# Second-layer modulation on VectorE: closing operations one to a place, the gates turned by PE and stored as rows, the first loads one chunk earlier in the program

## Chip, core and metric

One core of one Trainium2 chip runs the whole program. The metric is the device time of one execution in microseconds; the time before is the median of three runs. PE is the matrix engine, DVE is VectorE, ACT is ScalarE, POOL is GpSimd, SP is SyncE, whose queue issues nearly all DMAs here.

## The reference

A two-layer diffusion backbone: 1024 latent tokens and 256 context tokens of width 1024. Each layer is a mixer and a gated convolutional feed-forward network, each between norms whose shift, scale and gate come from a modulation vector:

```python
mod_lat = (jax.nn.silu(c) @ w_mod[l] + b_mod[l])[:, None, :]
mod_ctx = (jax.nn.silu(c_ctx) @ w_mod[l] + b_mod[l])[None, None, :]
sh1, sc1, g1, sh2, sc2, g2 = jnp.split(mod_lat, 6, axis=-1)
...
h_lat = rms_norm(x, norm_pre_ffn[l]) * (1.0 + sc2) + sh2
x = x + g2 * rms_norm(conv_ffn(h_lat, ...), norm_post_ffn[l])

def conv_ffn(h, w_up, conv_w, conv_b, w_down):
    u = depthwise_conv3(h @ w_up) + conv_b
    a, g = jnp.split(u, 2, axis=-1)
    return (jax.nn.silu(g) * a) @ w_down
```

The change is about the modulation of the second layer (l = 1): six vectors of 1024 for the latent tokens and the first two (shift and scale) for the context, 8192 dot products of length 1024.

## The kernel before

Matrix products are made in fp32 from split operands: each is a high and a low part in fp32r, and every product is three matmuls (high by high, low by high, high by low). The feed-forward network of the first layer (`ffn_up` with `ctx` true) runs over 22 chunks j = 0 to 21 of 128 hidden channels and their 128 gates. Its latent part is a 2x2 block product with 7 instead of 8 block products (S1 to S4 and T1 to T4 are sums of weight and token blocks), the context tokens are multiplied plainly (`u_pc`). In a chunk PE runs, in this order: the context product with A11 and A12; A12 (on B21); S2 (into `u_v`); the context product with A21 and A22; S1; S3; A22; A11 of the next chunk; and S4, which closes the chunk's `u_g`. VectorE adds the pieces up (`f_u`, then `u_v<-u_g`, which the S4 product waits for, then the second `u_v`), and makes the outer taps of the convolution; ScalarE makes the middle tap (`f_t`), the high parts of the weights and the silu; POOL makes the weight sums (`w_s`) and the low parts. Each finished chunk, `f_t` of 640 KB, is stored to DRAM (`actd`); there is one buffer per `f_t`, so that ScalarE's first middle tap of the context in the next chunk waits for that store.

Beside this, a generator, `mod_second`, makes the modulation of the second layer on VectorE. The context manager `in_order` holds the compute engines (PE, ACT, DVE, POOL) to the order in which the code is written; SP's DMAs are put in order by the framework's scheduler, up to chunk 21. `modulation(n)` takes n steps of the generator, and is called at fixed **places** of a chunk, seven in each of the chunks 1 to 21: one in `gate_end`, three after the sum `f_u`, one after each of the two context convolutions, one before the S4 product; and one more after the loop. In chunk 0 it takes none.

The generator's steps are: four loads of inputs (two rows `c_row`, the first two weight pieces `m_raw`) and three small tables; ScalarE's silu of the two rows; 128 jobs, each one product of a weight piece of 128x512 with the row, summed along it into one column of `m_acc` (the rows with L364), which also issues the load of the piece two jobs later into the buffer just read; then the sum of the two halves and the two bias sums in one step; and in the last step the copies and products that make the four tiles `mod_0`, `mod_1`, `mod_3`, `mod_4`, the gates `m_gate`, and two DMAs that write the gates, which lie across partitions, number by number to `gated` in DRAM. That is 132 steps, the last in chunk 19.

The next stage, `ffn_down`, multiplies by `w_down`; its first loads (`d_rawB`, `d_rawA`, `d_t`) are issued while the last chunks run. The second layer reads `mod` and `gated` much later.

Of the kernel before, what the change touches and what calls it, by code (L numbers as in the profile page):

```python
# [11 lines left out]
F32 = mybir.dt.float32  # L12
# [3 lines left out]
OP = mybir.AluOpType  # L16
# [4 lines left out]
P = 128  # L21
D = 1024
KT = D // P
# [26 lines left out]
def vap(t, off, dims):  # L50

    b = t[:]
    return bass.AP(tensor=b.tensor, offset=b.offset + off, ap=[list(b.ap[0])] + [list(d) for d in dims])
# [15 lines left out]
class Trunk:  # L69
# [255 lines left out]
                self.mod[l, kind] = m  # L325


    def mod_second(self, hp, sp):

        nc, a = self.nc, self.a  # L330
        raw, row = (hp.tile([P, 1024], F32, name=n, tag="n_t22", bufs=2) for n in ("m_raw", "c_row"))
# [40 lines left out]
            yield  # L372
        t = acc[:, 0]
        nc.vector.tensor_tensor(out=t, in0=t, in1=acc[:, 1], op=OP.add)
        nc.vector.tensor_tensor(out=t[:, :16], in0=t[:, :16], in1=bias[:, :16], op=OP.add)
        nc.vector.tensor_tensor(out=t[:, 16:], in0=t[:, 16:], in1=bias, op=OP.add)
        yield
        for kind in (0, 1, 3, 4):
            m = self.mod[1, kind] = self.cp.tile([P, KT, 2], F32, name=f"mod1_{kind}")
            for s in range(2 if kind < 2 else 1):  # L380
                src = t[:, (0 if s else 16) + KT * kind:][:, :KT]
                if kind in (1, 4):
                    w = pre[:, KT * (kind // 3):][:, :KT]
                    nc.vector.scalar_tensor_tensor(out=m[:, :, s], in0=src, scalar=1.0, in1=w, op0=OP.add, op1=OP.mult)
                else:
                    nc.vector.tensor_copy(m[:, :, s], src)
        nc.vector.tensor_tensor(out=gts, in0=vap(t, 16 + 2 * KT, ((3 * KT, 2), (1, KT))),
                                in1=post.rearrange("p (a b) -> p a b", a=2), op=OP.mult)
        for gi in range(2):
            nc.sync.dma_start(self.gated[1, gi, 0].rearrange("(k p) -> p k", p=P), gts[:, gi])  # L390


    def load_gates(self, l, gi, kinds, sp):
# [1186 lines left out]
    def ffn_up(self, l, src, ctx, x_src, x_dst, hp, pp, tp, es, ups, beside):  # L1580


        nc, a = self.nc, self.a
# [194 lines left out]
        with self.in_order(*self.compute, behind=l == 1), ExitStack() as loads:  # L1778
            sp, cw, sums = second_front() if l == 1 else up_front()

            down = iter(())
            mods = self.mod_second(hp, sp) if ctx else iter(())

            def modulation(n):
                for _ in range(n if j else 0):
                    next(mods, None)

            for j in range(FK):
# [79 lines left out]
                conv_start(t1[:, :SEQ], V, j + FK)  # L1868
                next(down, None)
                modulation(1)  # L1870
                product(Z, ("S4",), "B22", False, True)
                if "p1" in ahead:
                    st["p1"] = ahead.pop("p1")
# [1058 lines left out]
```

## Time and profile before

| what | value |
|---|---|
| median of three runs | 3279.52 us (3276.45 to 3287.17) |
| the profiled execution, whole | 3285.08 us |
| its span, first to last instruction | 3283.2 us |
| mean granted PE clock | 0.969 |
| first layer's up-projection, chunks 1 to 21 | about 1106 to 1635 us of the span |
| VectorE's 128 products for the modulation (L364) | 148.4 us busy, 1121.2 to 1568.6 us |
| packets under 512 B, whole execution | 26944 |

Times in rows of the profile are microseconds from the start of the span; a group's mean is in nanoseconds. In a row of the timeline the first number is the start, the second the duration; the brackets at its end hold how long the engine had been idle and what released it. "SPq" is a DMA issue of SP's queue, not the transfer. A row of the windows holds the stretch, its length, the busy time of PE, PE's weight load, DVE, ACT and POOL with the count of instructions, the granted clock, the DMA engines' mean busy share and GB/s.

### The profile page before, as it was taken

The numbers are of one execution on the slowest core, as the hardware profiler recorded it, in microseconds if no ns is written. First come the engines' busy times: TensorE is split into PE (matmuls) and PEld (weight loads), VectorE is DVE, ScalarE is ACT, GpSimd is POOL, SyncE is SP. The second block draws the span as 40 slices with busy tenths as digits, with TensorE's granted clock in tenths as the row PEclk, the third lists the DMA queues.
The fourth block names the chain that finished last, engine by engine and source line by source line (L and its number), as shares of the span: only waits on it lengthen the run. The fifth ranks groups of instructions, "written<-read, shape, count | busy, mean of one in ns | idle before, by whom it ended". The sixth has DMA issues, their size and how long they took to land.

```text
span 3283.2 us, 48708 instructions
## 1 busy us (share of the span) xinstructions
PE 3080.9 (94%) x18160; PEld 2551.2 (78%) x18160; DVE 2143.3 (65%) x3610; ACT 1506.6 (46%) x2693; POOL 1584.8 (48%) x1169
## 2 busy tenths in 40 slices
PE   7989999689998899999999989999998989999998
PEld 4867777478887688888788768889986768888787
DVE  4457666567775787878578652477775464555787
ACT  3323332366665444334344442566665543443443
POOL 1130111477773676776500111677775367777200
PEclk8999999699999899999999989999998989999999
DMA  7333112511114244444475672222224212222755
GB/s 251 110 101 119 41 37 64 180 30 63 58 55 155 87 146 156 141 140 149 124 250 200 224 226 108 70 64 63 61 72 163 91 64 84 78 89 84 252 195 180
DMA packets 212149, 396.13 MB, mean 121 GB/s; under 512 B 26944, under 2 KB 88896, under 8 KB 211912
## 3 DMA queue, kind: packets, MB, share of 16 engines
q1 hardware_dynamic: 202216, 359.46, 33.2%
q0 software_dynamic: 9696, 33.57, 2.6%
q8 instruction: 142, 2.33, 0.3%
q14 instruction: 95, 0.78, 0.1%
HBM read 314.28 MB, written 79.05 MB: 120 GB/s over the span
## 4 chain that ended last, share of the span: by engine, by line
PE 74%; DVE 11%; DMA 4%; ACT 4%; issue 4%; POOL 2%; SPq 0%; POOLq 0%; ACTq 0%; DVEq 0%
PE g_ps L139 20%; PE u_g L139 13%; PE d_ps L139 12%; PE u_v L139 10%; PE u_pc L139 3%; PE a_pv L139 2%; PE c_pv L139 2%; PE c_s L139 2%; PE c_pt L2560 2%; PE a_pt L1183 2%; DVE a_pl L1185 1%; PE o_ps L139 1%; PE a_s L139 1%; DMA d_rawB<-in_w_down 1%; DMA m_raw<-in_w_mod 1%
## 5 line engine op out<-in xcount | busy, mean ns | idle before, releaser
L147 POOL TENSOR_TENSOR rs_r<-rs_e,mhalf 128x1 f32<-128x1 f32 (+3 forms) x102 | 82.5, 810 | 839.3 <-DVE rs_e L146 422.6
L139 PE MATMUL d_ps<-d_Bl,d_Ah 128*128 128x512 f32 x704 | 276.7, 393 | 3.0 <-DVE d_Bl L1943 3.0
L139 PE MATMUL d_ps<-d_Bh,d_Ah 128*128 128x512 f32 x704 | 275.7, 392 | 2.9 <-ACT d_Bh L1942 1.5
L2543 POOL TENSOR_SCALAR c_p<-c_p,rl 128x640 f32<-128x640 f32 (+1 forms) x128 | 232.8, 1820 | 93.9 <-DVE rl L2542 62.4
L139 PE MATMUL d_ps<-d_Bh,d_Al 128*128 128x512 f32 x704 | 275.7, 392 | 1.5 <-DVE d_Al L1943 1.5
L1163 POOL TENSOR_SCALAR a_p<-a_p,rl 128x1280 f32<-128x1280 f32 (+1 forms) x80 | 242.2, 3030 | 62.6 <-DVE rl L1162 55.8
L139 PE MATMUL g_ps<-xh,w_hi 128*128 128x512 f32 (+1 forms) x640 | 257.0, 402 | 5.6 <-DVE hq L794 3.5
L139 PE MATMUL g_ps<-xh,w_lo 128*128 128x512 f32 (+1 forms) x640 | 238.0, 372 | 2.2 <-POOL w_lo L2443 2.2
L139 PE MATMUL g_ps<-xl,w_hi 128*128 128x512 f32 (+1 forms) x640 | 238.0, 372 | 0.0
L1185 DVE TENSOR_TENSOR a_pl<-a_pt,a_ph 128x512 fp32r<-128x512 f32 (+1 forms) x200 | 119.0, 602 | 88.1 <-ACT a_ph L1184 87.9
L364 DVE CUSTOM_DVE_ANT_0 m_raw<-m_raw,c_row 128x512 f32<-128x512 f32 x128 | 148.4, 1170 | 23.4 <-DMA m_raw<-in_w_mod 23.2
L1620 DVE TENSOR_TENSOR f_u<-u_v,f_p 128x512 f32<-128x512 f32 x88 | 60.4, 687 | 152.9 <-PE u_v L139 152.9
L139 PEld LDWEIGHTS d_ps<-d_Bl,d_Ah 128*128 128x128 f32 x704 | 132.8, 189 | 34.8 <-DVE d_Bl L1943 7.0
L139 PEld LDWEIGHTS d_ps<-d_Bh,d_Ah 128*128 128x128 f32 x704 | 132.8, 189 | 32.5 <-ACT d_Bh L1942 2.6
L1606 POOL TENSOR_TENSOR w_S4l<-w_s,w_S4h 128x512 fp32r<-128x512 f32 x44 | 57.2, 1301 | 207.5 <-ACT w_S4h L1605 207.5
L139 PEld LDWEIGHTS d_ps<-d_Bh,d_Al 128*128 128x128 f32 x704 | 132.9, 189 | 30.0 <-DVE d_Al L1943 2.9
L1184 ACT CAST a_ph<-a_pt 128x512 fp32r<-128x512 f32 (+1 forms) x200 | 102.0, 518 | 109.4 <-PE a_pt L1183 109.3
L2563 DVE TENSOR_TENSOR c_pl<-c_pt,c_ph 128x256 fp32r<-128x256 f32 (+1 forms) x256 | 113.0, 470 | 59.2 <-ACT c_ph L2562 58.0
L139 PE MATMUL g_ps<-w_hi,xh 128*128 128x512 f32 (+1 forms) x368 | 143.6, 390 | 5.5 <-DVE xh L2317 3.0
L139 PE MATMUL g_ps<-w_lo,xh 128*128 128x512 f32 (+1 forms) x368 | 138.2, 375 | 3.5 <-DVE w_lo L2304 2.4
L139 PEld LDWEIGHTS g_ps<-xh,w_lo 128*128 128x128 f32 x640 | 121.2, 189 | 25.2 <-POOL w_lo L2443 2.7
L139 PEld LDWEIGHTS g_ps<-xh,w_hi 128*128 128x128 f32 x640 | 121.6, 190 | 24.6 <-issue 7.6
(589 smaller groups left out, 10007.8 us busy)
## 6 DMA issues: line engine op xcount, KB each, us to landing
w_raw<-in_w_up SPq DMA_DIRECT2D x88, 512.0 KB
d_rawA<-actd SPq DMA_DIRECT2D x77, 512.0 KB
d_rawB<-in_w_down SPq DMA_DIRECT2D x74, 512.0 KB
m_raw<-in_w_mod SPq DMA_DIRECT2D x128, 256.0 KB
m_raw<-in_w_mod SPq DMA_DIRECT2D x48, 512.0 KB
actd<-f_t SPq DMA_DIRECT2D x22, 640.0 KB
actd<-f_t SPq DMA_DIRECT2D x22, 512.0 KB
vcd<-cv_st POOLq DMA_DIRECT2D x20, 512.0 KB, 2.9
```

The source lines that it names most:

```text
L139: return self.nc.tensor.matmul(out, lhsT, rhs, start=start, stop=stop, skip_group_check=True, **k)
L147: nc.gpsimd.tensor_tensor(out=r[:p, :n], in0=e[:p, :n], in1=self.mhalf[:p, :n], op=OP.pow)
L364: nc.vector.tensor_tensor_reduce(out=w, in0=w, in1=halves[1][n % 2], scale=1.0, scalar=0.0, op0=OP.mult, op1=OP.add, accum_out=acc[:, k, o ...
L1163: nc.gpsimd.tensor_scalar(Pt[:, :nk], Pt[:, :nk], rl, None, op0=OP.mult)
L1183: nc.tensor.transpose(pt[:, m, qt * P:(qt + 1) * P], Pt[:, kts[j + m] * P:(kts[j + m] + 1) * P], self.ident)
L1184: nc.scalar.copy(ph[:, j:j + n], pt[:, :n])
L1185: nc.vector.tensor_tensor(out=pl[:, j:j + n], in0=pt[:, :n], in1=ph[:, j:j + n].bitcast(F32), op=OP.subtract)
L1606: nc.gpsimd.tensor_tensor(out=lo, in0=part(j, name), in1=hi.bitcast(F32), op=OP.subtract)
L1620: nc.vector.tensor_tensor(out=out, in0=x, in1=y, op=OP.add)
L2543: nc.gpsimd.tensor_scalar(Pt[:, :n], Pt[:, :n], rl, None, op0=OP.mult)
L2560: nc.tensor.transpose(pt[:, j, :], Pt[:, (src + j) * P:(src + j + 1) * P], self.ident)
L2563: nc.vector.tensor_tensor(out=vap(pl, o, dims), in0=pt[:, :cnt], in1=vap(ph, o, dims).bitcast(F32), op=OP.subtract)
```

## The change

Four things. The two bias sums each get a step of their own, and so does each operation that makes the `mod` tiles; three of these tiles' copies go from VectorE to ScalarE. The gates are made first, turned by a PE transpose into a PSUM tile (`m_pt`), copied by ScalarE into a `c_row` buffer that is free by then, and stored as 16 rows of 128 numbers. And one step, the loads, is taken at the end of chunk 0. With it the generator has 141 steps after chunk 0, the last at the first place of chunk 21.

```diff
--- before.py
+++ after.py
@@ -325,7 +325,7 @@
                 self.mod[l, kind] = m
 
 
-    def mod_second(self, hp, sp):
+    def mod_second(self, hp, sp, tp):
 
         nc, a = self.nc, self.a
         raw, row = (hp.tile([P, 1024], F32, name=n, tag="n_t22", bufs=2) for n in ("m_raw", "c_row"))
@@ -372,22 +372,31 @@
             yield
         t = acc[:, 0]
         nc.vector.tensor_tensor(out=t, in0=t, in1=acc[:, 1], op=OP.add)
+        yield
         nc.vector.tensor_tensor(out=t[:, :16], in0=t[:, :16], in1=bias[:, :16], op=OP.add)
+        yield
         nc.vector.tensor_tensor(out=t[:, 16:], in0=t[:, 16:], in1=bias, op=OP.add)
         yield
+        nc.vector.tensor_tensor(out=gts, in0=vap(t, 16 + 2 * KT, ((3 * KT, 2), (1, KT))),
+                                in1=post.rearrange("p (a b) -> p a b", a=2), op=OP.mult)
+        yield
+        pt = tp.tile([P, 512], F32, name="m_pt", tag="n_pt", bufs=1)
+        nc.tensor.transpose(pt[:16, :P], gts.rearrange("p a b -> p (a b)"), self.ident)
+        yield
+        rows = halves[1][0][:16, :P]
+        nc.scalar.copy(rows, pt[:16, :P])
+        for gi in range(2):
+            nc.sync.dma_start(self.gated[1, gi, 0].rearrange("(k p) -> k p", p=P), rows[KT * gi:KT * gi + KT])
         for kind in (0, 1, 3, 4):
             m = self.mod[1, kind] = self.cp.tile([P, KT, 2], F32, name=f"mod1_{kind}")
             for s in range(2 if kind < 2 else 1):
                 src = t[:, (0 if s else 16) + KT * kind:][:, :KT]
+                yield
                 if kind in (1, 4):
                     w = pre[:, KT * (kind // 3):][:, :KT]
                     nc.vector.scalar_tensor_tensor(out=m[:, :, s], in0=src, scalar=1.0, in1=w, op0=OP.add, op1=OP.mult)
                 else:
-                    nc.vector.tensor_copy(m[:, :, s], src)
-        nc.vector.tensor_tensor(out=gts, in0=vap(t, 16 + 2 * KT, ((3 * KT, 2), (1, KT))),
-                                in1=post.rearrange("p (a b) -> p a b", a=2), op=OP.mult)
-        for gi in range(2):
-            nc.sync.dma_start(self.gated[1, gi, 0].rearrange("(k p) -> p k", p=P), gts[:, gi])
+                    nc.scalar.copy(m[:, :, s], src)
 
 
     def load_gates(self, l, gi, kinds, sp):
@@ -1779,7 +1788,7 @@
             sp, cw, sums = second_front() if l == 1 else up_front()
 
             down = iter(())
-            mods = self.mod_second(hp, sp) if ctx else iter(())
+            mods = self.mod_second(hp, sp, tp) if ctx else iter(())
 
             def modulation(n):
                 for _ in range(n if j else 0):
@@ -1868,6 +1877,8 @@
                 conv_start(t1[:, :SEQ], V, j + FK)
                 next(down, None)
                 modulation(1)
+                if j == 0:
+                    next(mods, None)
                 product(Z, ("S4",), "B22", False, True)
                 if "p1" in ahead:
                     st["p1"] = ahead.pop("p1")
```

What stands where after that. The first place is the start of chunk 1 on VectorE, from the product that closes chunk 0 (`f_t`, 128x1280); the rows L364 come in pairs, the product and the reading of its sum. Before:

```order
L1654 TENSOR_TENSOR f_t_11301<-f_t_11301,f_t_11300 128x1280
L1620 TENSOR_TENSOR f_u_11481<-u_v,f_p_11379 128x512
L364 ISA m_raw,m_acc<-m_raw,c_row 128x512
L364 ISA m_acc 128x1
L364 ISA m_raw,m_acc<-m_raw,c_row 128x512
L364 ISA m_acc 128x1
L1626 SCALAR_TENSOR_TENSOR f_t_11514<-u_pc,cw,f_t_11514 128x255
L1628 SCALAR_TENSOR_TENSOR f_t_11514<-u_pc,cw,f_t_11514 128x255
L364 ISA m_raw,m_acc<-m_raw,c_row 128x512
L364 ISA m_acc 128x1
L1626 SCALAR_TENSOR_TENSOR f_t_11513<-u_pc,cw,f_t_11513 128x255
L1628 SCALAR_TENSOR_TENSOR f_t_11513<-u_pc,cw,f_t_11513 128x255
```

and with the change:

```order
L1663 TENSOR_TENSOR f_t_11301<-f_t_11301,f_t_11300 128x1280
L1629 TENSOR_TENSOR f_u_11483<-u_v,f_p_11391 128x512
L364 ISA m_raw,m_acc<-m_raw,c_row 128x512
L364 ISA m_acc 128x1
L364 ISA m_raw,m_acc<-m_raw,c_row 128x512
L364 ISA m_acc 128x1
L364 ISA m_raw,m_acc<-m_raw,c_row 128x512
L364 ISA m_acc 128x1
L1635 SCALAR_TENSOR_TENSOR f_t_11516<-u_pc,cw,f_t_11516 128x255
L1637 SCALAR_TENSOR_TENSOR f_t_11516<-u_pc,cw,f_t_11516 128x255
L364 ISA m_raw,m_acc<-m_raw,c_row 128x512
L364 ISA m_acc 128x1
```

One product more stands ahead of the first context convolution (128x255), and all later ones have moved up by one place. SP's row for the loads of `c_row` and of the first two pieces is the same in both programs, behind the same four weight loads. On ScalarE the silu of the two rows stands ahead of the casts of w_A11h and w_A12h instead of behind them.

The second place is chunk 19 on VectorE, where the jobs end. Before, from the last product on:

```order
L364 ISA m_raw,m_acc<-m_raw,c_row 128x512
L364 ISA m_acc 128x1
L1626 SCALAR_TENSOR_TENSOR f_t_15458<-u_pc,cw,f_t_15458 128x255
L1628 SCALAR_TENSOR_TENSOR f_t_15458<-u_pc,cw,f_t_15458 128x255
L374 TENSOR_TENSOR m_acc<-m_acc 128x64
L375 TENSOR_TENSOR m_acc<-m_acc,m_tab 128x16
L376 TENSOR_TENSOR m_acc<-m_acc,m_tab 128x48
L1626 SCALAR_TENSOR_TENSOR f_t_15457<-u_pc,cw,f_t_15457 128x255
L1628 SCALAR_TENSOR_TENSOR f_t_15457<-u_pc,cw,f_t_15457 128x255
L386 COPY mod_0_15468<-m_acc 128x8 x2
L384 SCALAR_TENSOR_TENSOR mod_1_15471<-m_acc,m_tab 128x8 x2
L386 COPY mod_3_15474<-m_acc 128x8
```

then mod_4, m_gate and the three sums f_u, u_v, u_v. With the change:

```order
L374 TENSOR_TENSOR m_acc<-m_acc 128x64
L1635 SCALAR_TENSOR_TENSOR f_t_15459<-u_pc,cw,f_t_15459 128x255
L1637 SCALAR_TENSOR_TENSOR f_t_15459<-u_pc,cw,f_t_15459 128x255
L376 TENSOR_TENSOR m_acc<-m_acc,m_tab 128x16
L1635 SCALAR_TENSOR_TENSOR f_t_15458<-u_pc,cw,f_t_15458 128x255
L1637 SCALAR_TENSOR_TENSOR f_t_15458<-u_pc,cw,f_t_15458 128x255
L378 TENSOR_TENSOR m_acc<-m_acc,m_tab 128x48
L1629 TENSOR_TENSOR f_u_15488<-u_v,f_p_15312 128x512
L1629 TENSOR_TENSOR u_v<-u_g,f_u_15488 128x512
L1629 TENSOR_TENSOR u_v<-u_v,f_u_15488 128x512
L380 TENSOR_TENSOR m_gate<-m_acc,m_tab 128x16
```

The lump between the two convolutions and in front of f_u has become one small operation at each; the gates stand behind the sums that PE waits for. The rest on VectorE follows in chunk 20 (from its first context convolution; before, no row of the modulation was left there):

```order
L1635 SCALAR_TENSOR_TENSOR f_t_15674<-u_pc,cw,f_t_15674 128x255
L1637 SCALAR_TENSOR_TENSOR f_t_15674<-u_pc,cw,f_t_15674 128x255
L397 SCALAR_TENSOR_TENSOR mod_1_15648<-m_acc,m_tab 128x8
L1635 SCALAR_TENSOR_TENSOR f_t_15673<-u_pc,cw,f_t_15673 128x255
L1637 SCALAR_TENSOR_TENSOR f_t_15673<-u_pc,cw,f_t_15673 128x255
L397 SCALAR_TENSOR_TENSOR mod_1_15648<-m_acc,m_tab 128x8
L1629 TENSOR_TENSOR f_u_15704<-u_v,f_p_15525 128x512
```

and mod_4 in chunk 21, ahead of the convolution of `u_g`. On ScalarE the copies of `m_pt` and of mod_0 stand in chunk 20 between the casts of w_A12h and w_S2h, that of mod_3 ahead of the copy f_p. On PE the one new row, the transpose, stands in chunk 20 between the products A12 and S2. POOL's order is the same.

The third place is SP's queue around the gates' DMAs. Before:

```order
L349 DMA m_raw<-in_w_mod 128x512 x2
L1655 DMA actd<-f_t_15241 128x1280
L349 DMA m_raw<-in_w_mod 128x512
L1589 DMA w_raw<-in_w_up 128x1024
L390 DMA gated<-m_gate 128x8x1 x2
L1908 DMA d_rawB<-in_w_down 128x2x512
L1655 DMA actd<-f_t_15458 128x1280
L1908 DMA d_rawA<-actd 128x2x512
```

and with the change:

```order
L1598 DMA w_raw<-in_w_up 128x1024
L349 DMA m_raw<-in_w_mod 128x512 x2
L1664 DMA actd<-f_t_15243 128x1280
L1598 DMA w_raw<-in_w_up 128x1024
L1919 DMA d_rawB<-in_w_down 128x2x512
L389 DMA gated<-c_row 8x128 x2
L1664 DMA actd<-f_t_15459 128x1280
L1919 DMA d_rawA<-actd 128x2x512
```

The gates' two DMAs have gone from in front of the first load of `w_down` to behind it; they stay ahead of the store of chunk 19 (the first `actd` below them).

## The prediction

> **What bounds the kernel now.** I read the page first, for the engine that sets the end.
>
> ```profile
> PE 3080.9 (94%) x18160; PEld 2551.2 (78%) x18160; DVE 2143.3 (65%) x3610; ACT 1506.6 (46%) x2693; POOL 1584.8 (48%) x1169
> ```
>
> PE is busy 94% of the span, so an instruction of another engine costs time only where PE stands still for it. The change lies in the up-projection of the first layer. There I read the chain in order of time (start, length, what).
>
> ```profile
> 1159.06 2.87 PE u_pc L139 x24
> ...
> 1183.90 2.87 PE u_pc L139 x24
> ...
> 1592.13 11.29 DMA actd<-f_t
> ...
> 1611.16 2.87 PE u_pc L139 x24
> ...
> 1635.15 190.17 PE d_ps L139 x837
> ```
>
> The first row is the context product that opens chunk 3, the second that of chunk 4: a chunk is 24.84 us of PE. The third u_pc row opens chunk 21, 18 chunks after chunk 3. At 18 x 24.84 = 447.12 us it would stand at 1606.18; it stands at 1611.16. So **4.98 us are lost** between chunks 3 and 21, and the chain names a DMA of 11.29 us there. PE's timeline, taken in pieces from 1110 to 1615, shows where; the brackets hold PE's idle time and who ended it.
>
> ```profile
> 1130.12 0.50 PE L139 MATMUL u_g<-x_B220h,w_S4h 128*128 128x512 f32 x1 [0.26 <-DVE u_v L1620]
> 1156.04 0.50 PE L139 MATMUL u_g<-x_B220h,w_S4h 128*128 128x512 f32 x1 [0.79 <-DVE u_v L1620]
> 1580.57 0.50 PE L139 MATMUL u_g<-x_B220h,w_S4h 128*128 128x512 f32 x1 [1.95 <-DVE u_v L1620]
> 1608.14 0.50 PE L139 MATMUL u_g<-x_B220h,w_S4h 128*128 128x512 f32 x1 [2.39 <-DVE u_v L1620]
> ```
>
> These are the S4 products of chunks 1, 2, 19 and 20, each waiting for VectorE's sums. Chunks 3 to 18 show no idle at all. The last two, 4.34 us, are most of the 4.98; the rest is the restart after each. The places between are full, so the jobs themselves cost nothing today.
>
> **The closing lump, chunk 19.** VectorE's timeline there:
>
> ```profile
> 1572.31 0.99 DVE L374 TENSOR_TENSOR m_acc<-m_acc 128x64 f32<-128x64 f32 x1
> ...
> 1576.51 1.33 DVE L384 SCALAR_TENSOR_TENSOR mod<-m_acc,m_tab 128x8 f32<-128x8 f32 x2
> ...
> 1579.02 0.16 DVE L387 TENSOR_TENSOR m_gate<-m_acc,m_tab 128x16 f32<-128x16 f32 x1
> 1579.10 0.68 DVE L1620 TENSOR_TENSOR f_u<-u_v,f_p 128x512 f32<-128x512 f32 x1
> ```
>
> And the same stretch of the chunk before, where two products of the modulation stand in its place:
>
> ```profile
> 1547.46 1.22 DVE L364 CUSTOM_DVE_ANT_0 m_raw<-m_raw,c_row 128x512 f32<-128x512 f32 x1
> ...
> 1549.53 0.87 DVE L364 CUSTOM_DVE_ANT_0 m_raw<-m_raw,c_row 128x512 f32<-128x512 f32 x1
> ...
> 1551.09 0.69 DVE L1620 TENSOR_TENSOR f_u<-u_v,f_p 128x512 f32<-128x512 f32 x1 [0.69 <-PE u_v L139]
> ```
>
> In step with chunk 18 the sum f_u would start at 1551.09 + 24.84 = 1575.93; it starts at 1579.10, 3.17 us late, of which PE shows 1.95. Afterwards this chunk has one product less, the accumulator sum in that product's place, and one bias sum after each context convolution. A small operation took between 0.16 and about 1.3 us here, so I price each of the two at 1.3 us: from 1572.31, where the first pair of convolutions is done, plus 1.3, plus the second pair (0.48 each, as in the row at 1124.38 below), plus 1.3, gives f_u at 1575.87. That is in step, even at the dearest price. The 1.95 us go. The gate product stands behind the last sum PE waits for. In chunk 20 the two mod_1 operations take the same two places (2.6 us against 1.22 + 0.87 + 0.69 idle = 2.78): hidden. mod_4 stands in chunk 21 ahead of a convolution that waits for ScalarE anyway.
>
> **The gate's DMA, chunk 20.**
>
> ```profile
> 1579.20 1.00 SPq L390 DMA_DIRECT2D gated<-m_gate  x2
> DMA packets 2633, 1.70 MB, mean 68 GB/s; under 512 B 2128, under 2 KB 2128, under 8 KB 2632
> 1570.79 0.56 ACT L1623 ACTIVATE f_t<-u_pc,cw 128x256 f32<-128x256 f32 x1
> 1603.52 0.57 ACT L1623 ACTIVATE f_t<-u_pc,cw 128x256 f32<-128x256 f32 x1 [5.03 <-DMA actd<-f_t]
> ```
>
> Two issues of 4 KB write 2048 single numbers: in 1579 to 1604 the DMA view counts 2128 packets under 512 B. The 640 KB store of chunk 19 (on the chain at 1592.13) sits behind them for 11.29 us, ScalarE stands 5.03 us behind the store, and VectorE and PE behind ScalarE. A store without them:
>
> ```profile
> 1120.73 0.33 SPq L1655 DMA_DIRECT2D actd<-f_t  x1
> 1123.78 0.57 ACT L1623 ACTIVATE f_t<-u_pc,cw 128x256 f32<-128x256 f32 x1 [0.27 <-DMA actd<-f_t]
> ```
>
> It is down in 3.05 us. Afterwards the gates leave as 16 rows of 512 B, in SP's order behind a load of w_down and ahead of this store, ready some microseconds before it. The store, itself 1.95 us earlier, is issued at about 1590.2 and down at 1593.2; ScalarE needs it in step with its convolution of chunk 19 (1570.79 + 24.84) at 1595.6. The 2.39 us go too, with both restarts: **the term is -4.98 us**. The cover is 2.4 us wide; a landing time of 5.4 us would use it up, and every microsecond more would come back. Next late in chunk 20 is then nothing but PE. The row at 1635.15 says that what gained here is kept: 837 matmuls of the down-projection follow without a wait, and their loads are released by this stage's buffers.
>
> **What is added.**
>
> ```profile
> L296 PE MATMUL mod_pt<-ident,mod_rows 128*128 128x128 f32 x12 | 1.9, 282 | 0.7 <-ACT mod_rows L234 0.7
> 1565.57 0.62 ACT L1605 CAST w_S2h<-w_s 128x512 fp32r<-128x512 f32 x1 [3.02 <-POOL w_s L1599]
> ```
>
> One transpose on PE, in the full stretch of chunk 20: 0.16 us in a stream (1.9 / 12), 0.28 alone; I take **+0.28**. Its operand is a chunk's last fifth old by then, so it waits for nothing. The trace has no copy as small as ScalarE's four new ones; a 128x256 activation took 0.57 (row at 1603.52), so the copy out of PSUM and two of mod_0 are at most 1.7 us, and stand before w_S2h, where ScalarE idles 3.02: nothing. The fourth stands ahead of the copy f_p, behind which ScalarE waits for a convolution.
>
> **The loads a chunk sooner.** In SP's order the four loads keep their place, since the buffers that they fill are read until then; and
>
> ```profile
> 1115.00:1117.00 2.00, 2.00 (x15) 1.84 (x14) 0.80 (x1) 2.00 (x4) 0.25 (x1) 1.00 0.00 0
> 1117.61 1.15 ACT L344 ACTIVATE c_row<-c_row 128x512 f32<-128x512 f32 x2
> ```
>
> the DMA engines already stand empty before the first use. Worth nothing. What moves is each job, one place ahead: ScalarE's silu by two casts (the two products take 1.15 us, and POOL, which reads the casts next, has two sums to make first), and in chunk 1 a third product before the first context convolution.
>
> ```profile
> 1122.40 4.99 SPq L349 DMA_DIRECT2D m_raw<-in_w_mod  x3
> 1124.38 0.48 DVE L1626 SCALAR_TENSOR_TENSOR f_t<-u_pc,cw,f_t 128x255 f32<-128x255 f32 x1 [0.30 <-ACT f_t L1623]
> 1125.30 1.73 DVE L364 CUSTOM_DVE_ANT_0 m_raw<-m_raw,c_row 128x512 f32<-128x512 f32 x1
> 1139.35 1.58 DVE L364 CUSTOM_DVE_ANT_0 m_raw<-m_raw,c_row 128x512 f32<-128x512 f32 x1 [2.70 <-DMA m_raw<-in_w_mod]
> L364 DVE CUSTOM_DVE_ANT_0 m_raw<-m_raw,c_row x128: 680/1042/1807, 1121.2 to 1568.6; 128x512 f32<-128x512 f32 x128
> ```
>
> The last row has the product's shortest, median and longest time in ns. The third product's weights are issued at 1122.40. By the times of this stretch they are down some 2.3 us later, since VectorE took them at 1125.30 without a wait. It can start at about 1124.7 and ends near 1125.8, so the convolution comes 1.4 us later; a shorter wait in each later product gives part back, and I put chunk 1's S4 0.6 us later. Chunk 2's S4 is set by the wait at 1139.35, whose load stands behind a weight load on SP before and after, so it stays at 1156.04. PE has 0.79 us to spare there: 0.6 vanishes in it. From both sides: chunk 2's stall gone as well, -1.06 (its S4 comes 25.92 after that of chunk 1, against 24.84); or the last three products of chunk 1 at the longest, 1.81 us: 1124.7 + 3 x 1.81 + 4 x 0.48 + 2 sums of 0.7 = 1133.4, 3.3 later, of which chunk 2 has 0.79 and a restart of 0.3 to spare: +2.2. I take **+0.1**, near the rows of chunk 1 itself.
>
> The product took 0.87 us in chunk 18 and 1.73 in chunk 1. [...]
>
> **Sum.** -4.98 + 0.28 + 0.1 = -4.6 us. The profiled execution took 3285.08 us (span 3283.2 and 1.88 around it), so 3280.5; that execution was 5.56 above the median of the three runs, 3279.52, and against the median it is **3274.9**.
>
> **Rivals.**
> - *A wait takes the place of the DMA's* (0.12): the store still lands late in chunk 20, beside the first load of w_down, and only chunk 19's stall goes: -1.95, a restart of 0.32, + 0.28 + 0.1, about -1.9: 3277.6. For it: a load of 512 KB is issued ahead of the store. Against: it is the store's own 3.05 us that count by then, with 2.4 us of cover.
> - *Chunk 2 is relieved too* (0.12): the product in front of its convolution finds its weights earlier: -1.06 more, 3273.8. Against: SP's order there.
> - *Slower, the crowded second chunk* (0.05): the products stand one place closer to the start. If the six before chunk 2's S4 each wait for a POOL instruction and take 1.81 us instead of the median 1.04, its S4 comes 4.6 us later, and POOL, held by the last three of chunk 1 for as much (2.3 us), releases the weight load later that stands ahead of the wait at 1139.35: with PE's 0.79 spent, +6.1 in place of +0.1, net +1.4, 3280.9. It decides from a slip of 5.5 us in chunk 2. Against: chunks 3 to 18 run this very order without an idle PE.
> - *The change doesn't bring what it moves to PE's end* (0.05): the gain is waited for again at the end of the down-projection, where the chain is VectorE and DMA: 0, 3279.5. Against: those loads are released in order by what comes before.
>
> **How the numbers follow.** My forecast has 0.66. A measurement of this kernel can tell about 0.3%, 9.8 us, from no change, and every case is smaller. What falls outside comes from scatter: the three runs reach from 3.1 below to 7.7 above their median. From -4.6, another 5.2 us down makes it faster (0.08), 14 up slower (0.03); same 0.89. The range takes the rivals, 3273.8 to 3280.9, the dear end of chunk 1 (3277.0), and some 4 us of scatter around the middle of the cases: 3269 to 3283.
>
> **What would show it.** Right: no idle PE before the S4 products of chunks 19 and 20; u_pc rows 24.84 apart from chunk 3 to 20, and chunk 21's 25.1 after; some 2000 packets under 512 B fewer on the page; the store of chunk 19 down in 3 to 4 us; VectorE's small closing operations still up to 1.3 us each, but with f_u waiting for PE behind them. Wrong: idle PE over 1 us before S4 in chunk 1 or over 0.8 in chunk 2 beside full chunks 19 and 20 (the start gives it back); or ScalarE still waiting for actd in chunk 20.

## The result, and the profile after

| | before | this |
|---|---|---|
| median, 22 runs each | 3282.18 us (3274.78 to 3288.70) | 3276.26 us (3271.88 to 3283.20) |
| ratio | | 0.9985 (0.9979 to 0.9991) |
| profiled execution, whole / span | 3285.08 / 3283.2 us | 3275.59 / 3273.8 us |
| mean granted PE clock | 0.969 | 0.970 |

The ratio is -4.9 us (-3.0 to -6.9). The forecast was -4.6, and 3274.9 us against a median of 3279.52 in three runs. By the prediction's bound of 0.3% that is no change, though the interval leaves out zero. The spans differ by 9.4 us, but some 5 of these lie in front of chunk 0's S4 and behind the opening of chunk 21, where the two programs are nearly alike; I take them for scatter. So the comparison goes by stage.

The chain of waits of the changed kernel in order of time (start, length, what), in the stretch shown of before:

```profile
1156.58 2.87 PE u_pc L139 x24
...
1578.86 2.87 PE u_pc L139 x24
1581.73 2.75 PE u_g L139 x12
1584.48 0.11 PE m_pt L384
1584.59 2.77 PE u_v L139 x12
...
1603.85 2.87 PE u_pc L139 x24
...
1627.85 12.25 PE d_ps L139 x53
```

The first row opens chunk 3, the last u_pc row chunk 21: 447.27 us, where before took 452.10. The DMA of 11.29 us has left the chain, and so have all VectorE and ScalarE rows in front of 1603.85. The step from chunk 20 to 21, 1578.86 to 1603.85, is 24.99, with the transpose's 0.11 in it. The down-projection follows at 1627.85 without a wait.

PE's timeline, the S4 rows with an idle time in brackets, from chunk 0 on:

```profile
1102.53 0.47 PE L139 MATMUL u_g<-x_B220h,w_S4h 128*128 128x512 f32 x1 [1.61 <-DVE u_v L1629]
...
1127.73 0.50 PE L139 MATMUL u_g<-x_B220h,w_S4h 128*128 128x512 f32 x1 [0.76 <-DVE u_v L1629]
...
1153.56 0.50 PE L139 MATMUL u_g<-x_B220h,w_S4h 128*128 128x512 f32 x1 [0.65 <-DVE u_v L1629]
...
1624.86 0.47 PE L139 MATMUL u_g<-x_B220h,w_S4h 128*128 128x512 f32 x1 [1.61 <-DVE u_v L1629]
```

Chunks 19 and 20 are gone from the list. Chunk 1 waits 0.76 where it waited 0.26. Chunks 0 and 21 waited 1.61 before, too. VectorE's timeline in chunk 19 and, below the dots, in chunk 20:

```profile
1569.83 0.50 DVE L376 TENSOR_TENSOR m_acc<-m_acc,m_tab 128x16 f32<-128x16 f32 x1
...
1571.46 0.20 DVE L378 TENSOR_TENSOR m_acc<-m_acc,m_tab 128x48 f32<-128x48 f32 x1
1573.46 0.69 DVE L1629 TENSOR_TENSOR f_u<-u_v,f_p 128x512 f32<-128x512 f32 x1 [1.79 <-PE u_v L139]
...
1594.82 1.22 DVE L397 SCALAR_TENSOR_TENSOR mod<-m_acc,m_tab 128x8 f32<-128x8 f32 x1
...
1596.87 1.18 DVE L397 SCALAR_TENSOR_TENSOR mod<-m_acc,m_tab 128x8 f32<-128x8 f32 x1
1598.45 0.69 DVE L1629 TENSOR_TENSOR f_u<-u_v,f_p 128x512 f32<-128x512 f32 x1 [0.40 <-PE u_v L139]
```

In both chunks VectorE now waits for PE ahead of f_u. The two mod_1 operations cost 1.2 us each and still leave 0.40. Last, ScalarE's and SP's timelines in chunk 20, and the packets of the whole page:

```profile
1584.82 0.25 ACT L387 COPY c_row<-m_pt 16x128 f32<-16x128 f32 x1
1584.97 0.29 ACT L399 COPY mod<-m_acc 128x8 f32<-128x8 f32 x2
1587.62 0.62 ACT L1614 CAST w_S2h<-w_s 128x512 fp32r<-128x512 f32 x1 [2.36 <-POOL w_s L1608]
...
1593.31 0.56 ACT L1632 ACTIVATE f_t<-u_pc,cw 128x256 f32<-128x256 f32 x1
```

```profile
1585.09 0.64 SPq L389 DMA_DIRECT2D gated<-c_row  x2
1586.47 0.34 SPq L1664 DMA_DIRECT2D actd<-f_t  x1
```

```profile
DMA packets 210102, 396.15 MB, mean 121 GB/s; under 512 B 24880, under 2 KB 86848, under 8 KB 209864
```

The middle tap f_t at 1593.31 waits for nothing: the store of chunk 19, issued at 1586.47, was down by then. The small copies take 0.5 us out of an idle time of about 2.9. There are 26944 - 24880 = 2064 packets under 512 B fewer.

### The profile page after: what moved, and what is told of

The parts are those of the page before. It is cut to its first block, busy times and chain, and to the rows that moved or that the text cites. A ratio compares the mean times of both kernels' runs of the same rounds, so it can differ in the third digit from the quotient of the medians.

```text
span 3273.8 us, 48712 instructions
## 1 busy us (share of the span) xinstructions
PE 3077.4 (94%) x18161; PEld 2546.5 (78%) x18161; DVE 2142.2 (65%) x3607; ACT 1507.4 (46%) x2697; POOL 1585.9 (48%) x1169
## 2 busy tenths in 40 slices
DMA packets 210102, 396.15 MB, mean 121 GB/s; under 512 B 24880, under 2 KB 86848, under 8 KB 209864
## 4 chain that ended last, share of the span: by engine, by line
PE 56%; DVE 4%; DMA 2%; issue 2%; ACT 2%; POOL 1%; SPq 0%; POOLq 0%; ACTq 0%; DVEq 0%
PE u_g L139 14%; PE d_ps L139 12%; PE u_v L139 10%; PE g_ps L139 10%; PE u_pc L139 3%; PE c_pv L139 2%; PE c_s L139 2%; PE c_pt L2571 2%; PE o_ps L139 1%; DMA d_rawB<-in_w_down 1%; DMA d_rawA<-actd 0%; DVE d_Bl L1954 0%; DMA m_raw<-in_w_mod 0%; DVE x_t L1452 0%; DMA n_x<-x2d 0%
## 5 line engine op out<-in xcount | busy, mean ns | idle before, releaser
L364 DVE CUSTOM_DVE_ANT_0 m_raw<-m_raw,c_row 128x512 f32<-128x512 f32 x128 | 146.9, 1158 | 22.3 <-DMA m_raw<-in_w_mod 22.1
```

Source lines behind the costliest of these rows:

```text
L364: nc.vector.tensor_tensor_reduce(out=w, in0=w, in1=halves[1][n % 2], scale=1.0, scalar=0.0, op0=OP.mult, op1=OP.add, accum_out=acc[:, k, o ...
```

## The experiments

Two stretches of the stage hold nearly all that the change touches (only mod_4 falls into chunk 21, whose S4 waits 1.61 us in both kernels): the **start**, from the S4 product of chunk 0 to the u_pc that opens chunk 3, and the **closing**, from there to the u_pc that opens chunk 21. (Some expectations count the start from chunk 0's A22 product to chunk 2's S4; the 5.5 to 6.7 us between A22 and S4 of chunk 0, in which the programs are alike, are left out below.) In before, chunk 0's S4 stands at 1105.63, by the same view of its trace:

```profile
1105.63 0.47 PE L139 MATMUL u_g<-x_B220h,w_S4h 128*128 128x512 f32 x1 [1.61 <-DVE u_v L1620]
```

Release, start and closing are read from the one profiled execution of each kernel. "Release" is the time from chunk 0's S4 to SP's issue of the weight load that stands ahead of the m_raw load for which chunk 2 waits.

| kernel | whole, us | release | start | closing |
|---|---|---|---|---|
| before | 3282.18 (median) | 28.80 | 53.43 | 452.10 |
| this | 3276.26 (median) | 29.49 | 54.05 | 447.27 |
| spread only | 3288.28 | 28.98 | 53.67 | 456.13 |
| turned only | 3277.80 | 28.98 | 53.56 | 450.97 |
| loads only | 3277.11 | 29.84 | 54.22 | 451.14 |
| without the sooner loads | 3280.72 | 28.99 | 53.62 | 447.27 |
| nine transposes | 3283.34 | 29.47 | 57.18 | 448.13 |
| numbers on ScalarE's queue | 3283.01 | 29.50 | 54.05 | 449.99 |
| lump in a quiet place | 3274.02 | 29.47 | 54.00 | 447.28 |
| start relieved | 3276.52 (median of 12) | 29.00 | 52.59 | 447.27 |

Single whole times scatter by more than the effects, so the verdicts go by the stretches.

**Spread only.** The closing operations one to a place, but the gates still written number by number and no sooner loads.

```diff
--- this
+++ spread only
-        yield
-        pt = tp.tile([P, 512], F32, name="m_pt", tag="n_pt", bufs=1)
-        nc.tensor.transpose(pt[:16, :P], gts.rearrange("p a b -> p (a b)"), self.ident)
-        yield
-        rows = halves[1][0][:16, :P]
-        nc.scalar.copy(rows, pt[:16, :P])
         for gi in range(2):
-            nc.sync.dma_start(self.gated[1, gi, 0].rearrange("(k p) -> k p", p=P), rows[KT * gi:KT * gi + KT])
+            nc.sync.dma_start(self.gated[1, gi, 0].rearrange("(k p) -> p k", p=P), gts[:, gi])
...
-                if j == 0:
-                    next(mods, None)
```

> The kernel with the change, but the gates are stored number by number as before and the loads are not taken in chunk 0: the closing operations one to a place alone. Measured by the distance of the context products (u_pc) that open chunks 3 and 21: 452.10 us before, 447.27 with the change. Theory (the DMA sets the end of chunk 20, the lump's 1.95 us only add to it where the DMA does not): chunk 19 has no idle PE, but m_gate is now made in the first place of chunk 20, about 2 us later than before, so the 2048 numbers and the store of chunk 19 behind them end about 2 us later: chunk 20's S4 product waits 5 to 7 us and the distance is 453 to 455, longer than before although a stall is gone. Rival (the two stalls are two separate terms, -2.3 and -2.7): 449.8.

The closing took 456.13 us: 4.03 more than before, although the lump's stall is gone. SP's, ScalarE's and PE's rows from the timeline of this kernel:

```profile
1583.94 1.00 SPq L383 DMA_DIRECT2D gated<-m_gate  x2
1590.25 0.33 SPq L1658 DMA_DIRECT2D actd<-f_t  x1
```

```profile
1606.34 0.56 ACT L1626 ACTIVATE f_t<-u_pc,cw 128x256 f32<-128x256 f32 x1 [8.31 <-DMA actd<-f_t]
```

```profile
1610.96 0.79 PE L139 MATMUL u_g<-x_B220h,w_S4h 128*128 128x512 f32 x1 [6.25 <-DVE u_v L1623]
...
1616.25 0.41 PE L139 MATMUL u_pc<-x_ctx0h,w_A11h 128*128 128x256 f32 x1
```

The numbers leave 4.74 us later than before and the store earlier, so that less of their time is over when the store comes: 8.31 us of waiting instead of 5.03, and PE stands 6.25 us. The two stalls of before were therefore **not additive**: taking the lump apart gave back 2.3 us (1.95 of idle PE and 0.32 for the restart, half of 4.98 - 4.34), and the longer wait took 3.9. How much of the 3.9 comes from the later issue of the numbers, and how much from the lump's stall no longer covering a part of the DMA's, this run does not tell. On top comes the clock, which the expectation did not hold: behind the gap the granted clock was 0.50, and S4's twelve matmuls took 5.29 us to the next product, where before took 2.85 in chunk 20 (1608.14 to 1610.99): 2.4 us more, and the three make up the 4.03.

**Turned only.** Before, with the gates turned and stored as rows; the lump stays.

```diff
--- before
+++ turned only
+        yield
+        pt = tp.tile([P, 512], F32, name="m_pt", tag="n_pt", bufs=1)
+        nc.tensor.transpose(pt[:16, :P], gts.rearrange("p a b -> p (a b)"), self.ident)
+        yield
+        rows = halves[1][0][:16, :P]
+        nc.scalar.copy(rows, pt[:16, :P])
         for gi in range(2):
-            nc.sync.dma_start(self.gated[1, gi, 0].rearrange("(k p) -> p k", p=P), gts[:, gi])
+            nc.sync.dma_start(self.gated[1, gi, 0].rearrange("(k p) -> k p", p=P), rows[KT * gi:KT * gi + KT])
```

> The kernel before, but the gates are turned by PE, copied by ScalarE and stored as 16 rows; the closing operations stay in one lump in chunk 19, the loads where they were. Theory: the lump's stall stays (1.95 us idle before chunk 19's S4, the transpose falls into it), chunk 20 has none: distance of chunks 3 to 21 447.12 + 1.95 + 0.3 = 449.4, store of chunk 19 down in 3 to 4 us. Rival (the store is slow for the load of w_down ahead of it): ScalarE still waits for it, distance above 451.

Chunk 20's S4 no longer waits: the DMA's stall goes with the turning alone. The closing took 450.97 us, not the 449.4 expected. PE's timeline and windows in chunk 19 (a row of the windows ends in granted clock, DMA share, GB/s):

```profile
1575.09 0.28 PE L391 MATMUL m_pt<-ident,m_gate 128*16 128x128 f32 x1 [0.63 <-DVE m_gate L387]
1576.42 0.50 PE L139 MATMUL u_g<-x_B220h,w_S4h 128*128 128x512 f32 x1 [1.06 <-DVE u_v L1626]
...
1580.86 0.28 PE L139 MATMUL u_pc<-x_ctx0h,w_A11h 128*128 128x256 f32 x1
```

```profile
1576.00:1578.00 2.00, 1.58 (x5) 1.30 (x6) 1.07 (x2) 0.86 (x1) 0.00 (x0) 0.76 0.88 311
1578.00:1580.00 2.00, 2.00 (x6) 1.51 (x6) 1.59 (x2) 0.82 (x2) 0.00 (x0) 0.50 0.10 39
```

The lump's stall stands there about as expected, 1.7 us in two pieces with the transpose between them. What the expectation missed is again the half clock behind the gap: S4 took 4.44 us to the next product (1576.42 to 1580.86) instead of the 2.85 of before's chunk 20. These 1.6 us are as much as the whole excess. PE's timeline of before:

```profile
1610.99 0.28 PE L139 MATMUL u_pc<-x_ctx0h,w_A11h 128*128 128x256 f32 x1
```

**Loads only.** Before, with the one step taken at the end of chunk 0.

```diff
--- before
+++ loads only
                 modulation(1)
+                if j == 0:
+                    next(mods, None)
                 product(Z, ("S4",), "B22", False, True)
```

> The kernel before with only the one step taken in chunk 0; everything after moves up by one place. Theory: in the start +0.1 us (from the first A22 product of chunk 0 with x_T40l to chunk 2's S4 product 57.09 us before, 57.22 with the change); at the end the lump stands between the two context convolutions, early enough that chunk 19's S4 does not wait, and the gates leave some 3 us earlier; but SP's order now has the last load of w_up behind them. If the queue works in order, that load comes down only after the 2048 numbers, POOL's weight sum waits for it and ScalarE behind it, and chunk 20's S4 waits 4 to 6 us: distance 451.5 to 453.5. If only the store of chunk 19 is held up by the numbers, it is down 3 us earlier and the distance is 449.1.

The lump, one place earlier in the program, fits between the convolutions, and chunk 19's S4 waits for nothing. But behind the numbers, now issued at 1566.77, the next weight load is late, and POOL waits 10.31 us for it. POOL's and PE's timelines:

```profile
1588.95 1.28 POOL L1599 TENSOR_TENSOR w_s<-w_raw 128x512 f32<-128x512 f32 x1 [10.31 <-DMA w_raw<-in_w_up]
```

```profile
1586.57 0.56 PE L139 MATMUL u_pc<-x_ctx3l,w_A22h 128*128 128x256 f32 x1 [2.29 <-issue]
```

The closing took 451.14 us, just below the 451.5 to 453.5 that the theory of the held transfers gave, and far from the rival's 449.1. The way is not the one that was thought of, however, so that the nearness of the number is luck. PE did not stand in front of S4; it stood 2.29 us in the middle of a context product, with the granted clock at 0.50 behind it (1586.38 to 1589.79). For that wait the trace names no releaser. Its cause stays open. One candidate that was not tried is the transfer of the program's own instructions, which the page counts as "q8 instruction": two of its packets stand 30.5 us apart here (1560.90 and 1591.40) and 24.3 in the changed kernel (1565.98 and 1590.28). But the second comes only after PE runs again, so this is no proof.

The start holds more than its 54.22 says. Here chunk 1's S4 waits 1.93 us for VectorE, and chunk 2's does not wait at all:

```profile
1123.53 0.50 PE L139 MATMUL u_g<-x_B220h,w_S4h 128*128 128x512 f32 x1 [1.93 <-DVE u_v L1620]
```

**Without the sooner loads.** The change less its fourth part.

```diff
--- this
+++ without the sooner loads
                 modulation(1)
-                if j == 0:
-                    next(mods, None)
                 product(Z, ("S4",), "B22", False, True)
```

> The kernel with the change without the step in chunk 0; every job and closing operation one place later. Theory: start 57.1 us as before the change, against 57.22; distance of chunks 3 to 21 447.3 to 447.8 (ScalarE's copy now waits for a transpose that stands behind S1 on PE, some 1.4 us of the 2.4 us of cover). So the earlier loads bring nothing, and the whole gain is in the closing. Rival (the loads sooner are part of the gain): chunk 1 or 2 shows more idle PE than before the change, start above 57.5.

The closing is the same to the last digit, 447.27, and the start is 53.62 against 54.05. The sooner loads bring nothing beside the other three parts, and cost what the start shows, 0.4 us in this pair.

**Nine transposes.** The transpose made nine times into the same place.

```diff
--- this
+++ nine transposes
-        nc.tensor.transpose(pt[:16, :P], gts.rearrange("p a b -> p (a b)"), self.ident)
+        for _ in range(9):
+            nc.tensor.transpose(pt[:16, :P], gts.rearrange("p a b -> p (a b)"), self.ident)
```

> The kernel with the change, with the one transpose made nine times into the same place. Theory: each costs PE what it costs in a stream, 0.16 us, so the distance of chunks 3 to 21 grows from 447.27 by 8 x 0.16 = 1.3 us to 448.6. Rival (each costs its whole time of 0.27 us): 449.4.

The closing grew by 0.86 us for eight more, so one costs **0.11 us**, less than either figure; the chain's row m_pt says the same. The run's own time says something else: its start took 57.18, 3.1 more than the change. The program is the same up to there, so this is one execution falling out of step. VectorE's and PE's timelines in chunk 2:

```profile
1149.79 1.82 DVE L364 CUSTOM_DVE_ANT_0 m_raw<-m_raw,c_row 128x512 f32<-128x512 f32 x1 [1.11 <-DMA m_raw<-in_w_mod]
...
1154.16 1.39 DVE L364 CUSTOM_DVE_ANT_0 m_raw<-m_raw,c_row 128x512 f32<-128x512 f32 x1
```

```profile
1156.94 0.80 PE L139 MATMUL u_g<-x_B220h,w_S4h 128*128 128x512 f32 x1 [2.46 <-DVE u_v L1630]
```

In the changed kernel's profiled execution the same two products took 0.83 and 0.86, and S4 waited 0.65. This is the crowded second chunk, at about half the price that the prediction gave it; 1.4 of the 3.1 us are S4 at half clock behind the gap (4.24 us to the next product).

**Numbers on ScalarE's queue.** Spread as in the change and loads sooner, but the gates written number by number by DMAs that ScalarE issues, so that nothing on SP's queue stands behind them.

```diff
--- this
+++ numbers on ScalarE's queue
-        yield
-        pt = tp.tile([P, 512], F32, name="m_pt", tag="n_pt", bufs=1)
-        nc.tensor.transpose(pt[:16, :P], gts.rearrange("p a b -> p (a b)"), self.ident)
-        yield
-        rows = halves[1][0][:16, :P]
-        nc.scalar.copy(rows, pt[:16, :P])
         for gi in range(2):
-            nc.sync.dma_start(self.gated[1, gi, 0].rearrange("(k p) -> k p", p=P), rows[KT * gi:KT * gi + KT])
+            nc.scalar.dma_start(self.gated[1, gi, 0].rearrange("(k p) -> p k", p=P), gts[:, gi])
```

> The kernel with the change, but the gates are stored number by number again, without the transpose, through ScalarE's DMA queue instead of SP's, at the same place (end of chunk 19). Theory (the cost is that the store of chunk 19 stands behind the numbers in one queue): the store takes 3 to 6 us, ScalarE does not wait for it, distance of chunks 3 to 21 447.1 to 447.6. Rival (the numbers hold the DMA engines themselves, whatever the queue): the store is down only when the numbers are, 10 us or more after its issue, chunk 20's S4 waits 3 to 5 us, distance 450 to 452.

The rival was right in kind: the closing took 449.99, at the near edge of its range, and chunk 20's S4 waited 2.57 us instead of 3 to 5. ScalarE's and SP's timelines, the queues of the stretch 1584 to 1585, and three of the windows behind the store's issue:

```profile
1578.24 1.07 ACTq L383 DMA_DIRECT2D gated<-m_gate  x2
...
1600.20 0.57 ACT L1626 ACTIVATE f_t<-u_pc,cw 128x256 f32<-128x256 f32 x1 [4.83 <-DMA actd<-f_t]
```

```profile
1588.62 0.33 SPq L1658 DMA_DIRECT2D actd<-f_t  x1
```

```profile
q10 hardware_dynamic: 40, 0.00, 26.2%
```

```profile
1586.00:1588.00 2.00, 2.00 (x10) 1.68 (x9) 1.97 (x2) 0.72 (x2) 1.92 (x2) 1.00 0.00 0
...
1592.00:1594.00 2.00, 2.00 (x11) 1.67 (x10) 0.00 (x0) 0.00 (x0) 2.00 (x3) 1.00 0.84 41
1594.00:1596.00 2.00, 2.00 (x11) 1.65 (x10) 0.00 (x0) 0.62 (x1) 1.27 (x2) 1.00 0.93 46
```

and the same windows behind the store's issue in the changed kernel:

```profile
1586.00:1588.00 2.00, 2.00 (x13) 1.75 (x12) 1.05 (x2) 0.38 (x1) 2.00 (x2) 1.00 0.38 156
1588.00:1590.00 2.00, 2.00 (x19) 2.00 (x18) 0.08 (x1) 0.86 (x2) 2.00 (x2) 1.00 0.43 174
```

The store still takes 1588.62 to 1600.1, 11.5 us. Queue q10 holds the numbers, and its last 40 packets are recorded before 1585; from 1585 to 1588 nothing is on record at all. Yet the store that follows keeps the DMA engines 84 to 93% busy at 41 to 46 GB/s, where the changed kernel moves 156 to 174 at 38 to 43%. The store is thus not queued behind the numbers on its queue: it runs, slowly, after writes that the records show as gone. What slows it is not in the trace.

**Lump in a quiet place.** As the change, but all ten closing operations on VectorE and in one step, at the last place of chunk 19, behind the sums that PE waits for. The turning of the gates follows it.

```diff
--- this
+++ lump in a quiet place
+        yield
+        yield
+        yield
         t = acc[:, 0]
         nc.vector.tensor_tensor(out=t, in0=t, in1=acc[:, 1], op=OP.add)
-        yield
         nc.vector.tensor_tensor(out=t[:, :16], in0=t[:, :16], in1=bias[:, :16], op=OP.add)
-        yield
         nc.vector.tensor_tensor(out=t[:, 16:], in0=t[:, 16:], in1=bias, op=OP.add)
-        yield
...
-                    nc.scalar.copy(m[:, :, s], src)
+                    nc.vector.tensor_copy(m[:, :, s], src)
```

> The kernel with the change, but all ten closing operations in one step on VectorE, at the last place of chunk 19, behind the sums that PE waits for and where POOL has little to do; copies on VectorE again; gates turned as in the change. Theory (what the lump cost was its place: ahead of the sums, and beside POOL, whose running instruction each small operation waited for): no idle PE in chunk 19 or 20, distance 447.3, and the ten operations take about 2 to 3 us together instead of 6.6, most of them 0.15 to 0.25 us each. Rival (they cost about 1 us each by themselves, and one to a place is what hides them): again 6 us, VectorE's convolution behind them is late, and the distance is above 448.

The closing took 447.28: the same gain. VectorE's timeline there, with POOL's last instruction of the stretch below it:

```profile
1573.01 0.61 DVE L377 TENSOR_TENSOR m_acc<-m_acc 128x64 f32<-128x64 f32 x1
1573.65 0.17 DVE L378 TENSOR_TENSOR m_acc<-m_acc,m_tab 128x16 f32<-128x16 f32 x1
...
1574.44 0.17 DVE L389 TENSOR_TENSOR m_gate<-m_acc,m_tab 128x16 f32<-128x16 f32 x1
1574.52 1.28 DVE L1634 SCALAR_TENSOR_TENSOR f_t<-u_v,cw,f_t 128x1023 f32<-128x1023 f32 x1
```

```profile
1572.24 1.29 POOL L1614 TENSOR_TENSOR w_A22l<-w_raw,w_A22h 128x512 fp32r<-128x512 f32 x1
```

All ten take 1.5 us (1573.01 to 1574.52). Before, VectorE spent 1572.31 to 1579.10 on them and one pair of convolutions. The first ends about when POOL's instruction does (1572.24 + 1.29 = 1573.53), the others run at 0.2 us once POOL is still. The place is what counts, not the one-to-a-place. This place differs from the old one in two ways, though: it is beside a still POOL, and it is behind the sums that PE waits for. The run does not tell which of the two the gain needs.

**Start relieved.** The change, with one product fewer in chunk 1 behind the sums, none at chunk 2's first place, and the sum of the halves and the two bias sums in one step, so that the closing keeps its place.

```diff
--- this
+++ start relieved
-            def modulation(n):
+            def modulation(n, gate=False):
+                if ctx and (j, n) == (1, 3):
+                    n = 2
+                if ctx and j == 2 and gate:
+                    n = 0
                 for _ in range(n if j else 0):
                     next(mods, None)
...
         def gate_end(j):
-            modulation(1)
+            modulation(1, True)
...
-        yield
         nc.vector.tensor_tensor(out=t[:, 16:], in0=t[:, 16:], in1=bias, op=OP.add)
-        yield
```

> The kernel with the change, with no job in the third place of chunk 1 and none in the first place of chunk 2 (the two that stand ahead of VectorE's late sums), all later jobs and closing operations up to two places later, both bias sums in one step. Theory: chunk 1's S4 waits 0 to 0.3 us instead of 0.76, chunk 2's not at all instead of 0.65; start 55.9 us instead of 57.22, distance of chunks 3 to 21 447.3 as with the change: another -1.3 us, ratio to before about 0.9981. Rival (something else is late in chunk 2, the store of chunk 1 or POOL's sums): chunk 2's S4 still waits over 0.4 us.

The stage does what was wanted: start 52.59, 1.46 us better than the change, closing 447.27. In time it can't be told apart: 0.9984 (0.9974 to 0.9993) of before, beside 0.9985 (0.9979 to 0.9991). Its interval leaves out 1, so it beats the kernel before; that it beats the change is not shown.

## Why the prediction held, and where it did not

**The closing** was forecast at -4.98 + 0.28 = -4.70 and measured at 447.27 - 452.10 = -4.83. Each sign that the prediction named is there: no idle PE in chunks 19 and 20, 24.99 us from chunk 20 to 21 (25.1 forecast), 2064 packets fewer, the small operations at up to 1.22 us with f_u waiting for PE behind them, a store that ScalarE does not wait for. The experiments show that the term needs both parts of the change: the spread alone gives +4.03, the turning alone -1.13, both together -4.83. The lump in a quiet place shows that the spread can be replaced by a better place.

**The transpose** was put at 0.28, the length of its row when alone, and costs 0.11.

**The start** is the step that failed in size: "+0.1 us" forecast, +0.6 measured against the one trace of before and about +0.5 by the means of several kernels. The start is 54.00 to 54.22 in four kernels with the sooner loads and 53.43 to 53.67 in four without (means 54.08 and 53.57); the fifth with them is the execution of 57.18. Chunk 1 went as forecast: its S4 came 25.20 us after that of chunk 0, where before took 24.49, so 0.7 later against 0.6. What failed is the sentence that chunk 2's S4 "stays at 1156.04". The load for which chunk 2 waits stands behind a weight load on SP, as the prediction said; but that weight load waits for POOL, and POOL was held up in chunk 1. POOL's timelines, of before and of the change, at the same place:

```profile
1125.18 1.29 POOL L1606 TENSOR_TENSOR w_S2l<-w_s,w_S2h 128x512 fp32r<-128x512 f32 x1
```

```profile
1122.27 1.74 POOL L1615 TENSOR_TENSOR w_S2l<-w_s,w_S2h 128x512 fp32r<-128x512 f32 x1
```

and VectorE's third product of chunk 1 in the changed kernel:

```profile
1122.16 0.70 DVE L364 CUSTOM_DVE_ANT_0 m_raw<-m_raw,c_row 128x512 f32<-128x512 f32 x1 [0.99 <-DMA m_raw<-in_w_mod]
```

Beside the added product POOL's instruction takes 1.74 instead of 1.29. In the four kernels of the table without sooner loads and in the relieved one it took 1.27 to 1.29, and the release stood at 28.80 to 29.00; in four with them it took 1.74 to 1.82 and the release stood at 29.47 to 29.50. So some 0.5 to 0.7 us of POOL's go to SP's weight load, to the m_raw load behind it, and to chunk 2: in the kernels where chunk 2's S4 waits, it comes 21.5 to 21.7 us after the release, but for the execution of 57.18.

In these ten traces the instruction that started second, by a hair, was the slower one. In the four kernels with 1.74 to 1.82, VectorE's third product of chunk 1 started 0.03 to 0.11 us before POOL's w_S2l and took 0.69 to 0.70. In the other six, w_S2l started 0.06 to 0.13 us before the product, and the product took 1.70 to 1.77. The kernel with the loads alone is of this second kind: its added product took 1.77 (from 1116.96, w_S2l from 1116.90), so its loss is VectorE's, in chunk 1, where S4 came 26.36 us after that of chunk 0, 1.9 later than in before and not 0.6. Its release is late all the same, 29.84, with two later instructions of POOL at 1.71 and 1.75 (w_s, from 1121.54 and 1125.23) in place of 1.29: 0.9 of the 1.0 that it is behind before's. POOL's delay is the mechanism of the prediction's slower rival at a tenth of its price; the prediction had it in hand for the rival and left it out of the sum.

**The dear end of chunk 1.** The +2.2 was not met: the last three products of chunk 1 took 0.69 to 0.87 us here, not 1.81. That one of the two engines is slower beside the other shows in the quiet lump (operations of 0.2 us beside a still POOL; up to 1.2 beside a busy one in the changed kernel) and in POOL's 1.74 instead of 1.29; which of them it was hung on 0.03 to 0.13 us here. Neither came near +2.2: the start is 54.05 where VectorE went first and 54.22 with the loads alone, where POOL did, against 53.43 in before.

**The numbers' DMA.** That the turning takes the DMA's stall away was right, and the cover of the store was wide enough. The picture behind it, a store that "sits behind them" in the queue, was not: on another queue the store took as long, 11.5 us against 11.29.

**The rivals.** No other wait took the place of the DMA's. Chunk 2 was not relieved by the change; the last experiment shows what that would be worth. The gain reached the end, as far as 22 runs can tell: the stage says -4.83 + 0.5 = -4.3, the ratio -4.9 (-3.0 to -6.9). That the sum of -4.6 lies between the two is partly luck: the transpose was priced 0.17 too high and the start 0.4 to 0.5 too low. So is the nearness of 3274.9 to the 3276.26 measured, since the median of before that it starts from came out 2.7 higher with 22 runs. (The stall of chunk 2, priced at 1.06 for the rival, is 25.92 - 24.84 = 1.08; nothing hangs on it.)

## What to carry to other kernels

When several short operations stall an engine, ask first which engine is busy beside them and what waits behind them, and move the lump to a place where that engine is still and nothing urgent follows; here that did as much as taking it apart (447.28 and 447.27 us). A store of single numbers is to be judged by what has to be moved behind it, for 22 to 24 us here, on its own queue or another, not by its own few KB. Where work is added beside an engine whose instructions take longer for it (1.74 us instead of 1.29 here), follow the lateness of that engine through the buffers that it releases, a stage further than the stretch in which the two meet.

## What the runs showed of the hardware that was not expected

**2048 writes of single numbers were felt for 22 to 24 us**, whether the transfer that suffered was issued 3 or 13 us behind them. From the numbers' issue to the landing of the transfer that suffered: before, 1579.20 to 1603.4 with a store issued 12.9 us behind; spread only, 1583.94 to 1606.3 with a store 6.3 us behind; on ScalarE's queue, 1578.24 to 1600.1 with a store 10.4 us behind; loads only, 1566.77 to about 1588.9 with a load 2.9 us behind.

**The granted clock fell to half after short gaps.** It was 0.50 after PE gaps of 0.63 and 1.06 us close together (turned only), after 2.46 (nine transposes) and 2.29 (loads only), and stayed at 1.00 after 1.95 and 2.39 in before and after 2.57 in numbers on ScalarE's queue. Behind the gap S4 took 4.44 us (turned only), 4.24 (nine transposes) and 5.29 (spread only, after 6.25) instead of 2.85: 1.4 to 2.4 us more. So stalls of 1.7 to 2.6 us cost up to nearly twice their length here (1.69 and 1.6 on top in turned only), or hardly more than their length (2.57 in numbers on ScalarE's queue, whose closing is 2.72 behind that of the change).

No run was made to tell the two cases apart, but the traces go some way. In before and in the changed kernel the granted clock changes 35 and 37 times over the span, and any two of these changes lie a whole multiple of 3.41 us apart; the half clock lasted from 1577.06 to 1580.47 in turned only, from 1156.46 to 1159.87 in nine transposes and from 1586.38 to 1589.79 in loads only, 3.41 us each time. Counting PE's idle time inside each step of 3.41 us at full clock, from the end of chunk 0 to the end of chunk 21: the clock fell behind steps with 1.89 us of it (the changed kernel, 1100.22 to 1103.63), 1.97 (nine transposes) and 2.10 (loads only), and not behind steps with 1.76, 1.61 and 1.49 (before, from 1606.38, 1630.28 and 1579.08) or 1.61 (the changed kernel, from 1622.45). The gap of 2.57 us lay across two steps, as about 1.2 and 1.4, that of 2.39 as 0.63 and 1.76. The exception is turned only, where a step with 1.69 us was enough; 0.28 us of transpose lie between its two gaps, and if they count as idle it has 1.97. That they do is not shown. Nor does the sum tell the cases apart outside this stretch: earlier in the changed kernel the clock fell behind steps with 1.38 us (605.29 to 608.71) and 1.69 us (1083.15 to 1086.56).
